# Splitting the input projection's weights in the transfers: two loads from the GpSimd queue, one rounding and one accumulating, in place of one load, casts and subtractions

## Chip, cores and metric

The kernel runs on 1 core of a Trainium2 chip. The metric is the device time of one execution in microseconds (us), the median of several. A profile of one execution stands beside the times.

## What is computed

One layer of a diffusion backbone, for 128 context tokens and 512 latent tokens of width 1024. All arithmetic is float32. What matters here is the first product of the token-mixing part:

```python
p = h @ w_in                       # (640, 1024) x (1024, 5664)
qkv, z, beta, a, sc, gates = jnp.split(p, SPLITS, axis=-1)
qkv = silu(conv_centred(qkv, conv_qkv, n_rows))
q, k, v = heads(...)               # 8 heads of 64, q and k normalised
o_f, s_f = gated_delta_chunked(q, k, v, beta[0], g[0], s0[:, 0])
o_b, s_b = gated_delta_chunked(fl(q), fl(k), fl(v), fl(beta[1]), fl(g[1]), s0[:, 1])
y_b = (bg * conv_centred(cg * xs, conv_sc, n_rows)) @ w_br_b
m = sigmoid(ga) * y_a + sigmoid(gb) * y_b
```

The chunked DeltaNet needs, for each chunk of 64 tokens, the inverse of a triangular matrix (`triangular_solve`), and then a scan over the chunks. After the mixing come an output projection and a SwiGLU network.

## The kernel before

**Products in two parts.** TensorE multiplies in a rounded float32 (`F32R`). To keep precision, each operand is split into a high part (the rounded value) and a low part (the rest, rounded too), and each product is made of three matmuls: high times high, high times low, low times high (`mm3`, lines 83 to 85).

**The input projection** has 45 weight tiles of 1024 x 128 (512 KB each). `load_w` (line 61) brings one tile into a raw buffer `wr` by a transfer from the queue of SyncE (SP). `split` (line 49) makes `wh` on ScalarE (ACT) by a cast and `wl` on VectorE (DVE) by subtracting `wh` from the raw tile, in two halves of 512 columns each: per tile two casts (line 57) and two subtractions (line 58). Both stand at a raised priority (offset 200000). There are two buffers each for `wr`, `wh` and `wl`. `gemm_cm` then multiplies the tile with the 640 tokens, in two halves of 320 tokens with 8 steps of depth and 3 matmuls each, 48 matmuls per tile. Tile 0 holds the columns for the decay (`gates`); `qkv`, `zgate`, `short` and `gate_th` use the other 44.

**The DeltaNet** works on 4 pairs of heads, one after the other. `prepare` (from line 407) normalises q and k, makes the factors and masks, and inverts the triangular matrices: on DVE, 30 dependent steps of a product (`otmp`, line 556) and a subtraction (`X`, line 558) on 32 x 32 blocks, then two transposes (`RT` and `R`, lines 562 and 563), whose results TensorE multiplies (line 575). GpSimd (POOL) makes masks (`em`, `ea`), scaled tiles (`qh`, `kl`), and fills the tiles `KU`, `RS` and `AQ` by elementwise work and by transfers of its own queue (lines 459 to 536). `scan` (from line 598) then goes over the chunks, with small matmuls from `KU`, `RS`, `EW` (line 640) and `AQ` (line 670).

**The order.** A scheduler places every instruction on its engine's queue by priority. `scan` has the highest (offset 300000), then the splits (200000), then `prepare` (1000), and the projection's tiles fill TensorE in between. Each engine works through its queue in order; an instruction that waits holds up all that stand behind it.

Of the kernel before, what the change touches and what calls it, by code (L numbers as in the profile page):

```python
# [9 lines left out]
F32 = mybir.dt.float32  # L10
F32R = mybir.dt.float32r
I32 = mybir.dt.int32
AF = mybir.ActivationFunctionType
ALU = mybir.AluOpType
# [4 lines left out]
P = 128  # L19
D = 1024  # L20
KT = D // P
# [16 lines left out]
class Kernel:  # L38
    def __init__(self, ctx, tc, ins, outs, dbg=None):
        self.tc, self.nc, self.ctx = tc, tc.nc, ctx  # L40
        self.I, self.O = ins, outs
        self.dbg = dbg or (lambda name, ap: None)


    def urgent(self):
# [15 lines left out]
    def load_w(self, src, shape, pool=None, urgent=True):  # L61
        raw = self.rpool.tile(shape, F32, name="wr", tag="wr", bufs=self.nraw)
        self.nc.sync.dma_start(out=raw, in_=src)
        return self.split(raw, shape, "w", pool, urgent=urgent)

    def rsqrt(self, out, x, pool, n, tag):

# [321 lines left out]
    def qkv(self, p, hT):  # L389

        nc = self.nc
        out = []
        for j in (1, 0, 2):
            w = self.load_w(self.I["w_in"][1 + 3 * p + j], [P, KT, P])
            i = 4 * j + p
            y = self.da.tile([P, TOK], F32, name="cm", tag="cm", bufs=4)
            for h in range(2):
                ps = self.gemm_cm(w, hT, h)
                o = h * HALF
                with self.urgent():  # L400
                    nc.scalar.activation(out=y[:, o:o + HALF], in_=ps, func=AF.Copy, scale=self.taps[:, 1, i:i + 1])
                    self.conv(ps, self.taps, i, y, o, 5, h == 0)
            nc.scalar.activation(out=y, in_=y, func=AF.Silu)
            out.append((j, y))
        return [y for _, y in sorted(out, key=lambda a: a[0])]


    def prepare(self, p, qkv):
        nc, dn, dc, g = self.nc, self.da, self.dc, self.g
        mm = nc.tensor.matmul  # L410
# [277 lines left out]

    def zgate(self, p, hT):
        nc = self.nc  # L690
        w = self.load_w(self.I["w_in"][13 + p], [P, KT, P])
        for h in range(2):
            s = slice(h * HALF, (h + 1) * HALF)
            ps = self.gemm_cm(w, hT, h)
            with self.urgent():
                nc.scalar.activation(out=self.zf[:, p, s], in_=ps, func=AF.Silu)

    def short(self, i, hT):
        nc = self.nc
        ab = self.ab  # L700
        wc = self.load_w(self.I["w_in"][17 + 3 * i], [P, KT, P])
        cx = ab.tile([P, TOK], F32, name="cx", tag="dt", bufs=2)
        y = ab.tile([P, TOK], F32, name="cy", tag="dt", bufs=2)
        for h in range(2):
            ps = self.gemm_cm(wc, hT, h)
            with self.urgent():
                nc.scalar.copy(out=cx[:, h * HALF:(h + 1) * HALF], in_=ps)
        wx = self.load_w(self.I["w_in"][18 + 3 * i], [P, KT, P])
        for h in range(2):
            s = slice(h * HALF, (h + 1) * HALF)  # L710
            ps = self.gemm_cm(wx, hT, h)
            with self.urgent():
                nc.vector.tensor_tensor(out=cx[:, s], in0=cx[:, s], in1=ps, op=ALU.mult)
        nc.vector.tensor_scalar(out=y, in0=cx, scalar1=self.tapsc[:, 1, i:i + 1], scalar2=None, op0=ALU.mult)
        self.conv(cx, self.tapsc, i, y, 0, 10, True)
        wb = self.load_w(self.I["w_in"][19 + 3 * i], [P, KT, P])
        for h in range(2):
            s = slice(h * HALF, (h + 1) * HALF)
            ps = self.gemm_cm(wb, hT, h)
            with self.urgent():  # L720
                nc.vector.tensor_tensor(out=y[:, s], in0=y[:, s], in1=ps, op=ALU.mult)  # L721
        nc.sync.dma_start(out=self.ybd[i], in_=y)

    def gate_th(self, i, hT):

        nc = self.nc
        w = self.load_w(self.I["w_in"][29 + i], [P, KT, P])
        t = self.ab.tile([P, TOK], F32, name="gt", tag="dt", bufs=2)
        for h in range(2):
            ps = self.gemm_cm(w, hT, h)  # L730
            with self.urgent():
                nc.scalar.activation(out=t[:, h * HALF:(h + 1) * HALF], in_=ps, func=AF.Tanh, scale=0.5)
        nc.sync.dma_start(out=self.thd[i], in_=t)
# [695 lines left out]
```

## Time and profile before

| | us |
|---|---|
| median of 3 runs | 1089.32 |
| lowest and highest run | 1086.92, 1091.1 |
| the profiled execution, its own time | 1085.4 |
| its span | 1083.6 |
| TensorE (PE) busy | 1024.1 |
| VectorE (DVE) busy | 835.8 |
| ScalarE (ACT) busy | 484.4 |
| GpSimd (POOL) busy | 138.9 |

The span runs from the first to the last instruction; 1.8 us of the execution lie around it. Busy times are unions of an engine's instructions. Matmuls are pipelined, so that a busy TensorE is not one at its peak. A wait is put down to the instruction that ended last before the waiting one could start. The input projection runs from 42 to 514 us of the span.

### The profile page before, as it was taken

To read this page: it belongs to the slowest core of one execution; us is meant where nothing else is said; L and a number is where in the kernel's file an instruction comes from. 1 tells how busy PE (TensorE), PEld (TensorE's weight loads), DVE (VectorE), ACT (ScalarE), POOL (GpSimd) and SP (SyncE) were. 2 spreads that over 40 slices of the span, in tenths; PEclk is the share of its full clock that TensorE was granted. 3 is DMA by queue.
4 is the path that set the end of the run, shared out by engine and by line. 5 is a ranking of instruction groups with operands and counts; after the bars stand their busy time and mean duration, and the time that the engine had idled before them with its cause. 6 is when DMAs were issued, how large, how long until landed. Compare 5 with 4: busy or idle time off the path is not lost.

```text
span 1083.6 us, 19702 instructions
## 1 busy us (share of the span) xinstructions
PE 1024.1 (95%) x7729; PEld 929.0 (86%) x7729; DVE 835.8 (77%) x1698; ACT 484.4 (45%) x929; POOL 138.9 (13%) x168
## 2 busy tenths in 40 slices
PE   6999978988988989999998998999999999999997
PEld 3699978887887888899996887999999999788885
DVE  5767896997898897995995789888777775975336
ACT  5568436417524324434223466444445444623321
POOL 2215321062062150101000000000000000000000
PEclk9999989998998999999998998999999999999999
DMA  9435712264164276547953532323222222552214
GB/s 343 147 91 135 206 52 67 72 152 113 42 164 125 68 171 202 182 151 246 318 167 116 185 108 89 103 85 98 94 79 78 98 81 76 177 173 96 81 39 156
DMA packets 47399, 141.52 MB, mean 131 GB/s; under 512 B 9517, under 2 KB 10034, under 8 KB 47306
## 3 DMA queue, kind: packets, MB, share of 16 engines
q1 hardware_dynamic: 42746, 127.10, 36.1%
q0 software_dynamic: 4560, 13.15, 5.4%
q8 instruction: 61, 1.00, 0.4%
q14 instruction: 32, 0.26, 0.1%
HBM read 117.57 MB, written 12.18 MB: 120 GB/s over the span
## 4 chain that ended last, share of the span: by engine, by line
PE 69%; DVE 14%; DMA 2%; ACT 2%; issue 2%; SPq 0%; DVEq 0%; POOL 0%; ACTq 0%
PE acc L1163 21%; PE d L84 7%; PE d L85 7%; PE d L83 7%; PE acc L84 6%; PE acc L83 6%; PE acc L85 6%; PE d L1163 3%; DVE X L558 3%; PE s L640 2%; DVE otmp L556 2%; DVE wl L58 1%; PE v L611 1%; PE v L670 1%; DMA ea<-scr 1%
## 5 line engine op out<-in xcount | busy, mean ns | idle before, releaser
L83 PE MATMUL d<-hT,wh 128*128 128x320 f32 x720 | 227.8, 317 | 1.2 <-DVE cy L721 1.1
L84 PE MATMUL d<-hT,wh 128*128 128x320 f32 x720 | 228.6, 318 | 0.0
L85 PE MATMUL d<-hT,wl 128*128 128x320 f32 x720 | 227.8, 317 | 0.4 <-DVE wl L58 0.4
L57 ACT CAST wh<-wr 128x512 fp32r<-128x512 f32 x150 | 87.8, 618 | 143.2 <-PE d L84 74.4
L83 PEld LDWEIGHTS d<-hT,wh 128*128 128x128 f32 x720 | 137.3, 191 | 3.9 <-DVE cy L721 1.7
L85 PEld LDWEIGHTS d<-hT,wl 128*128 128x128 f32 x720 | 137.3, 191 | 3.2 <-issue 0.7
L84 PEld LDWEIGHTS d<-hT,wh 128*128 128x128 f32 x720 | 137.1, 191 | 2.9 <-issue 0.3
L58 DVE TENSOR_TENSOR wl<-wr,wh 128x512 fp32r<-128x512 f32 x150 | 104.2, 717 | 36.4 <-ACT wh L57 35.2
L1163 PE MATMUL acc<-mh,wl 128*128 128x320 f32 x280 | 86.9, 310 | 1.8 <-DVE wl L1098 1.8
L83 PE MATMUL acc<-wh,as 128*128 128x512 f32 x220 | 85.7, 390 | 2.1 <-ACT as L1297 2.1
L1163 PE MATMUL acc<-mh,wh 128*128 128x320 f32 x280 | 87.0, 311 | 0.3 <-ACT early L1177 0.3
L196 DVE SCALAR_TENSOR_TENSOR gacc<-wr,cv,gacc 128x1024 f32<-128x1024 f32 x64 | 80.1, 1278 | 9.1 <-DMA wr<-in_w_mod_dram 7.2
L1163 PE MATMUL acc<-ml,wh 128*128 128x320 f32 x280 | 86.7, 310 | 0.0
L84 PE MATMUL acc<-wl,as 128*128 128x512 f32 x220 | 85.6, 389 | 0.0
L85 PE MATMUL acc<-wh,as 128*128 128x512 f32 x220 | 85.5, 389 | 0.0
L1102 ACT CAST wh<-wr 128x512 fp32r<-128x512 f32 x66 | 40.6, 622 | 72.0 <-PE acc L1163 37.0
L1102 ACT CAST wh<-S 128x512 fp32r<-128x512 f32 x88 | 54.1, 619 | 36.4 <-PE d L1163 19.6
L1098 DVE TENSOR_TENSOR wl<-S,wh 128x512 fp32r<-128x512 f32 x88 | 60.0, 686 | 3.9 <-ACT wh L1102 3.0
L1098 DVE TENSOR_TENSOR wl<-wr,wh 128x512 fp32r<-128x512 f32 x66 | 45.3, 689 | 19.1 <-ACT wh L1102 18.2
L1163 PEld LDWEIGHTS acc<-mh,wl 128*128 128x128 f32 x280 | 52.8, 188 | 2.1 <-DVE wl L1098 2.0
L1163 PEld LDWEIGHTS acc<-mh,wh 128*128 128x128 f32 x280 | 52.7, 188 | 0.6 <-ACT early L1177 0.6
L1163 PEld LDWEIGHTS acc<-ml,wh 128*128 128x128 f32 x280 | 52.8, 189 | 0.0
(365 smaller groups left out, 2348.9 us busy)
## 6 DMA issues: line engine op xcount, KB each, us to landing
wr<-in_w_ffn_in_dram SPq DMA_DIRECT2D x48, 512.0 KB, 3.7
wr<-in_w_in_dram SPq DMA_DIRECT2D x45, 512.0 KB, 3.5
wr<-in_w_mod_dram SPq DMA_DIRECT2D x32, 512.0 KB, 4.0
wr<-in_w_ffn_out_dram SPq DMA_DIRECT2D x22, 512.0 KB, 3.4
mr<-in_w_mod_dram SPq DMA_DIRECT2D x16, 512.0 KB, 8.5
thd<-gt SPq DMA_DIRECT2D x16, 320.0 KB, 4.1
bth<-thd SPq DMA_DIRECT2D x16, 320.0 KB, 3.0
wr<-in_w_br_dram SPq DMA_DIRECT2D x8, 512.0 KB, 6.9
```

Source lines behind the costliest of these rows:

```text
L57: (high or nc.scalar.copy)(out=hi[:, s], in_=raw[:, s])
L58: (low or nc.vector).tensor_tensor(out=lo[:, s], in0=raw[:, s], in1=hi[:, s].bitcast(F32), op=ALU.subtract)
L83: mm(out, lhsT=ah, rhs=bh, start=start, stop=False)
L84: mm(out, lhsT=ah, rhs=bl, start=False, stop=False)
L85: mm(out, lhsT=al, rhs=bh, start=False, stop=stop)
L196: nc.vector.scalar_tensor_tensor(out=acc[v], in0=w, scalar=self.cv[:, k, v:v + 1], in1=acc[v], op0=ALU.mult, op1=ALU.add)
L556: nc.vector.tensor_tensor(out=t, in0=B[:, j + 1:32, j:j + 1].broadcast_to([P, n, j]), in1=X[:, j:j + 1, 0:j].broadcast_to([P, n, j]), op=A ...
L558: nc.vector.tensor_tensor(out=X[:, j + 1:32, 0:j], in0=X[:, j + 1:32, 0:j], in1=t, op=ALU.subtract)
L640: mm(ps[half(c2), o:o + 64], lhsT=w(d, c2, t, hd), rhs=R[:, d, c2, t, hd, :], start=True, stop=True)
L1098: tt = lambda o, a, b, op: nc.vector.tensor_tensor(out=o, in0=a, in1=b, op=op)
L1102: nc.scalar.copy(out=dst[0], in_=src)
L1163: nc.tensor.matmul(ps, lhsT=A[x][:, k], rhs=B[y][:, k], start=start and k == 0 and n == 0, stop=k == 3 and n == 2, skip_group_check=True)
```

## The change

44 of the 45 weight tiles of the input projection (all but tile 0) come through a new function `load_parts`. It issues three instructions per tile:

1. a transfer from POOL's queue that reads the float32 weights and writes them rounded, as `wh` (called HI below);
2. on ACT, `wl` = -`wh`, one instruction of 1024 columns;
3. a second transfer from POOL's queue, that reads the same weights again and adds them into `wl` (called LO below).

The raw buffers are no longer needed for this, so every third tile puts its two parts into the two `wr` buffers: three pairs of buffers are in turn, where there were two.

```diff
@@ -40,6 +40,7 @@
         self.dbg = dbg or (lambda name, ap: None)
+        self.turn = itertools.count(1)
@@ -62,6 +63,17 @@
         return self.split(raw, shape, "w", pool, urgent=urgent)
+
+    def load_parts(self, src):
+
+        nc = self.nc
+        tags = ("wh", "wl") if next(self.turn) % 3 else ("wr", "wr")
+        hi, lo = (self.wpool.tile([P, KT, P], F32R, name=name, tag=tag) for name, tag in zip(("wh", "wl"), tags))
+        with self.tc.high_priority(offset=200000):
+            nc.gpsimd.dma_start(out=hi, in_=src)
+            nc.scalar.activation(out=lo, in_=hi.bitcast(F32), func=AF.Copy, scale=-1.0)
+            nc.gpsimd.dma_start(out=lo, in_=src, accum_op=ALU.add)
+        return hi, lo
@@ -391,7 +403,7 @@
-            w = self.load_w(self.I["w_in"][1 + 3 * p + j], [P, KT, P])
+            w = self.load_parts(self.I["w_in"][1 + 3 * p + j])
@@ -688,7 +700,7 @@
-        w = self.load_w(self.I["w_in"][13 + p], [P, KT, P])
+        w = self.load_parts(self.I["w_in"][13 + p])
@@ -698,14 +710,14 @@
-        wc = self.load_w(self.I["w_in"][17 + 3 * i], [P, KT, P])
+        wc = self.load_parts(self.I["w_in"][17 + 3 * i])
...
```

`...` stands for the same replacement in the rest of `short` and in `gate_th`. Lines behind `load_parts` stand 12 further down in the new file.

**DVE in the inversion of the third pair of heads.** Each row is one instruction of DVE's queue; `wl<-wr,wh` is a subtraction of the split. Before:

```order
L556 TENSOR_TENSOR otmp<-blk,X 128x210
L558 TENSOR_TENSOR X<-X,otmp 128x10x21
L556 TENSOR_TENSOR otmp<-blk,X 128x198
L58 TENSOR_TENSOR wl<-wr,wh 128x512
L558 TENSOR_TENSOR X<-X,otmp 128x9x22
L58 TENSOR_TENSOR wl<-wr,wh 128x512
L556 TENSOR_TENSOR otmp<-blk,X 128x184
L558 TENSOR_TENSOR X<-X,otmp 128x8x23
```

and now:

```order
L570 TENSOR_TENSOR X<-X,otmp 128x10x21
L697 SCALAR_TENSOR_TENSOR zf<-v,onorm,zf 128x640
L568 TENSOR_TENSOR otmp<-blk,X 128x198
L570 TENSOR_TENSOR X<-X,otmp 128x9x22
L568 TENSOR_TENSOR otmp<-blk,X 128x184
L570 TENSOR_TENSOR X<-X,otmp 128x8x23
```

The subtractions of the split are gone from between the dependent steps; other work of DVE (here `zf`) stays there.

**POOL where the scan of the first pair ends and the tiles of the second are filled.** `KU`, `RS` and `AQ` are the tiles that the scan reads; `wh<-in_w_in_dram` is HI, `wl<-in_w_in_dram` is LO. Before:

```order
L459 TENSOR_TENSOR KU<-ident,egl 64x640 x4
L471 DMA KU<-kl 64x2x640
L625 MEMSET RS 64x128 x2
L472 DMA RS<-bv 64x2x640
L471 DMA KU<-kl 64x2x640
L472 DMA RS<-bv 64x2x640
L490 DMA AQ<-qtT 64x5x64 x8
L536 DMA AQ<-ea 64x2x640 x2
```

and now:

```order
L73 DMA wh<-in_w_in_dram 128x1024
L75 DMA wl<-in_w_in_dram 128x1024
L73 DMA wh<-in_w_in_dram 128x1024
L75 DMA wl<-in_w_in_dram 128x1024
L471 TENSOR_TENSOR KU<-ident,egl 64x640 x4
L483 DMA KU<-kl 64x2x640
L637 MEMSET RS 64x128 x2
L484 DMA RS<-bv 64x2x640
L73 DMA wh<-in_w_in_dram 128x1024
L483 DMA KU<-kl 64x2x640
L484 DMA RS<-bv 64x2x640
L502 DMA AQ<-qtT 64x5x64
```

Loads of weight tiles now stand ahead of this work and in the midst of it. The first `KU` here waits for TensorE's last use of it in the scan, as before, and a HI and a LO stand behind that wait.

**POOL in the last tiles of the projection.** A HI and the LO behind it belong to one tile (buffers number n and n + 1). Before, POOL's queue had no load of weights here. Now:

```order
L73 DMA wh_5245<-in_w_in_dram 128x1024
L75 DMA wl_5246<-in_w_in_dram 128x1024
L73 DMA wh_5344<-in_w_in_dram 128x1024
L75 DMA wl_5345<-in_w_in_dram 128x1024
L73 DMA wh_5403<-in_w_in_dram 128x1024
L75 DMA wl_5404<-in_w_in_dram 128x1024
```

Each LO stands straight behind its own HI, and the next tile's HI behind that LO. A HI waits until TensorE has done with the tile three before it; a LO waits for ACT, and ACT for the HI's data.

## Rows read from the trace of the kernel before

**Rows 1.** The page: the line of the span, and part 1.
```profile
span 1083.6 us, 19702 instructions
...
PE 1024.1 (95%) x7729; PEld 929.0 (86%) x7729; DVE 835.8 (77%) x1698; ACT 484.4 (45%) x929; POOL 138.9 (13%) x168
```

**Rows 2.** Busy time by stretch; columns: stretch, length, engines, granted clock, DMA share, GB/s.
```profile
42.00:102.00 60.00, 59.44 (x435) 57.42 (x435) 40.82 (x94) 45.33 (x72) 17.40 (x18) 1.00 0.44 118
102.00:168.00 66.00, 57.70 (x422) 55.66 (x422) 62.06 (x147) 28.26 (x47) 22.77 (x23) 0.95 0.41 116
168.00:250.00 82.00, 72.40 (x864) 64.99 (x859) 70.67 (x165) 33.57 (x68) 21.59 (x25) 1.00 0.42 105
250.00:334.00 84.00, 76.29 (x870) 69.22 (x864) 72.24 (x172) 40.96 (x75) 26.06 (x30) 0.93 0.42 107
334.00:405.00 71.00, 66.62 (x843) 59.68 (x840) 61.64 (x138) 27.76 (x58) 25.06 (x29) 0.96 0.43 115
405.00:462.00 57.00, 56.23 (x681) 49.33 (x676) 47.66 (x77) 24.05 (x55) 3.81 (x5) 1.00 0.56 183
462.00:514.00 52.00, 51.97 (x350) 50.65 (x349) 39.38 (x48) 20.36 (x37) 5.68 (x7) 1.00 0.60 201
sum 472.00, PE 440.64 PEld 406.95 DVE 394.49 ACT 220.28 POOL 122.38; mean PE 62.95 PEld 58.14 DVE 56.36 ACT 31.47 POOL 17.48
```

**Rows 3.** Waits of PE, 42 to 514 us: total, times, longest.
```profile
PE v L575 <- DVE RT L562: 9.6, 4, 4.5
PE w L479 <- DVE kh L448: 7.4, 3, 5.9
PE v L670 <- DVE RS L644: 5.3, 3, 2.6
```

**Rows 4.** Groups of DVE and of ACT by form, 42 to 514 us.
```profile
L58 DVE TENSOR_TENSOR wl<-wr,wh 128x512 fp32r<-128x512 f32 x92 | 66.3, 737 | 13.9 <-ACT wh L57 13.2
...
L57 ACT CAST wh<-wr 128x512 fp32r<-128x512 f32 x91 | 54.2, 617 | 70.9 <-PE d L84 53.4 <-issue 9.2 <-DVE cy L721 4.3
```

**Rows 5.** Chain of waits, 42 to 514 us: shares by line, then single pieces.
```profile
by line: PE d L84 12.0%; PE d L85 11.5%; PE d L83 11.4%; DVE X L558 5.9%; PE s L640 5.2%; DVE otmp L556 4.8%; DVE wl L58 3.3%; issue 2.3%; PE v L611 2.2%; PE v L670 1.9%; DMA ea<-scr 1.8%; DVE RT L562 1.7%; DMA AQ<-ea 1.4%; PE w L528 1.3%; 
...
119.67 6.62 DMA AQ<-ea
...
152.42 0.63 ACT wh L57
...
407.53 1.14 ACT wh L57 x2
```

**Rows 6.** Busy time by stretch of the instructions that touch wl alone.
```profile
42.00:102.00 60.00, 35.88 (x116) 21.68 (x116) 11.87 (x16) 1.00 0.44 118
102.00:168.00 66.00, 34.97 (x108) 21.12 (x108) 10.70 (x14) 0.95 0.41 116
168.00:250.00 82.00, 33.32 (x106) 19.90 (x106) 9.52 (x14) 1.00 0.42 105
250.00:334.00 84.00, 33.80 (x105) 20.71 (x105) 9.87 (x14) 0.93 0.42 107
334.00:405.00 71.00, 29.28 (x91) 17.50 (x91) 8.47 (x12) 0.96 0.43 115
...
462.00:514.00 52.00, 34.56 (x112) 21.11 (x113) 9.20 (x14) 1.00 0.60 201
```

**Rows 7.** DMA issues: count, size, median us from issue to landing.
```profile
wr<-in_w_in_dram SPq DMA_DIRECT2D x45, 512.0 KB, 3.5
...
RS<-bv POOLq DMA_DIRECT2D x8, 320.0 KB, 5.7
...
x1d<-yt POOLq DMA_DIRECT2D x5, 512.0 KB, 3.2
```

**Rows 8.** POOL: issue time of one transfer (min/median/max), and its waits.
```profile
L1063 POOL DMA_DIRECT2D x1d<-yt x5: 532/534/577, 609.0 to 645.4; - x5
...
POOL KU L459 <- PE s L640: 93.9, 3, 36.1
```

More of the change, by code (lines that the diff above doesn't have):

```diff
@@ L707, in short @@
                 nc.scalar.copy(out=cx[:, h * HALF:(h + 1) * HALF], in_=ps)
-        wx = self.load_w(self.I["w_in"][18 + 3 * i], [P, KT, P])
+        wx = self.load_parts(self.I["w_in"][18 + 3 * i])
         for h in range(2):
@@ L715, in short @@
         self.conv(cx, self.tapsc, i, y, 0, 10, True)
-        wb = self.load_w(self.I["w_in"][19 + 3 * i], [P, KT, P])
+        wb = self.load_parts(self.I["w_in"][19 + 3 * i])
         for h in range(2):
@@ L726, in gate_th @@
         nc = self.nc
-        w = self.load_w(self.I["w_in"][29 + i], [P, KT, P])
+        w = self.load_parts(self.I["w_in"][29 + i])
         t = self.ab.tile([P, TOK], F32, name="gt", tag="dt", bufs=2)
```

## The prediction

> **What bounds the kernel now.** I read the page's first part first [rows 1]: TensorE is busy for 95% of the span. The change touches only the input projection, which runs from 42 to 514 us, so I cut that into stretches [rows 2]. The reader is to see two things there. TensorE is busy for 440.6 of these 472 us, which leaves 31.4 us of idle time as the most that better feeding could return, the clock apart. And the idle time lies in four stretches, from 102 to 405 us: 8.3, 9.6, 7.7 and 4.4 us (length less PE busy). These are the stretches in which DVE is busiest (62.1 of 66, 70.7 of 82, 72.2 of 84, 61.6 of 71 us); before and behind them TensorE is full.
>
> Next I asked what TensorE waits for [rows 3]. The three largest waits end on DVE, 22.3 us in all: on `RT`, the end of the inversion, on `kh`, and on `RS` in the scan. They are not waits for weights. So the weights' subtractions cost time only by standing in DVE's queue among the steps that lead to `RT` and `kh`. The chain of waits [rows 5] tells how much of them is on the path: 3.3% of 472 us.
>
> **What the change takes away.** The subtractions are 92 of 737 ns in the window [rows 4]; 88 belong to the changed tiles, 64.9 us of DVE. The 88 casts at 617 ns are 54.3 us of ACT. In the four stretches the subtractions take 10.7, 9.5, 9.9 and 8.5 us [rows 6], each more than TensorE's idle time there. But they are not all on the path: on the chain there are 3.3% of 472 us = 15.6 us of subtractions, and five pieces of casts, 0.5 to 1.1 us, 3.5 us together (the first and the last are in rows 5). I take these 19.1 us as the gain, and not the 38.6 us of all subtractions in the four stretches, since DVE itself has 3.9, 11.3, 11.8 and 9.4 us without work there: other releasers than DVE's load come next. What is late then is the inversion's own steps (`X` 5.9% and `otmp` 4.8% of the chain), which stay.
>
> **What it adds.** ACT: 44 negations of 1024 columns. The nearest row is the cast of 512 columns, 617 ns [rows 4], so 0.62 to 1.23 us each; I take 1.2, or 53 us. It stands in for 54.3 us and cancels. The cover is ACT's own slack: 220 of 472 us busy [rows 2].
>
> POOL: 88 issues. The nearest are its own transfers of a 128 x 1024 tile, 0.53 us [rows 8], together 47 us on an engine that is busy for 122 of 472 us. The raw loads leave SP's queue; its other transfers can only come earlier for it, which I price at nothing.
>
> The supply of weights is what could fail, since one POOL queue now does it in series. Per tile: HI from issue to landing, the negation, the issue of LO; only then comes the next HI. For HI the nearest row is the same tile loaded from SP's queue, 3.5 us, or 3.2 us for a tile of that size issued by POOL [rows 7]. So 3.5 + 1.2 + 0.5 = 5.2 us per tile if LO's landing lies wholly beside the next HI. If the next HI has to wait until LO is in, LO's landing comes on top. No row shows an accumulating transfer. The nearest by size is 3.2 to 3.5 us; the nearest that reads SBUF as LO must (`RS`, 320 KB, from POOL's queue) takes 5.7 us [rows 7]. So the series takes 5.2 to 8.7 us with the first, up to 10.9 us with the second.
>
> What TensorE wants is read from the matmuls with `wl`, 16 per tile [rows 6]: 7.0 tiles in the last stretch, or one per 7.4 us; 7.25 tiles in the first, one per 8.3 us; one per 9.8 us in the second; one per 12.4, 12.8 and 12.5 us in the next three. I take 7 us, the middle between 5.2 and 8.7, which is faster than any of these; even 8.7 us would cost 7.0 x 1.3 + 7.25 x 0.4, less one tile's lead of 7.4 us, or 5 us. I put down 3 us.
>
> Here a rule speaks against the change. The Trainium skill (Collectives: The Full Stack, "The bandwidth ceiling: the fold count and why AG ≠ RS ≠ AR") says that an add in the transfer path needs two source reads, and that reducing so runs at about half the rate of copying (62.28 against 32.35 GB/s there). By it LO would take up to twice a plain load's transfer, and the sum would be that of the supply rival below; no run here shows it yet.
>
> POOL's other work: `KU` stood in its queue waiting 93.9 us for the scan in three waits [rows 8], with everything behind it held. Loads now stand ahead of it, and a HI and a LO behind it; with three pairs of buffers two tiles are ahead, 25 us at the pace of that stretch, so I price this wait at nothing. The transfers to `RS` and `AQ`, which the next scan reads, come later by the loads between them. I put down 1 us; nothing bounds it but the rival below.
>
> **The sum.** Against the profiled execution's 1085.4 us: - 15.6 - 3.5 + 3 + 1 = 1070.3 us. The median of the runs lies 3.9 us above that execution, so **1074 us** as a median. From 514 us on TensorE's work is the same in the same order; I change nothing there.
>
> **The rivals.**
>
> *The path moves to POOL and the transfers; no change.* Between pairs of heads the chain runs through POOL: `AQ` is filled from `ea`, a transfer that takes 6.6 us [rows 5], then `ea` is loaded anew, and DVE waits for it. These transfers now stand in POOL's queue behind a HI that waits for TensorE, or a LO that waits for a landing. One landing of 3.5 us at each of four pairs gives back 14 us: 1085.4 - 19.1 + 14 + 3 + 3.9 = 1087 us. For it speaks that DVE already has idle time in these stretches; against it, that the scheduler puts most loads where POOL would have waited anyway.
>
> *The supply is too slow; slower.* If LO holds up the next HI for 5.7 us, the series takes 10.9 us. Then TensorE waits in the full stretches: 7.0 x (10.9 - 7.4) = 24.5 us in the last, less the one tile of lead, 7.4; 7.25 x 2.6 = 18.9 us in the first; 6.75 x 1.1 = 7.4 us in the second; nothing in the next three. Together 43.4 us, and 1085.4 - 19.1 + 43.4 + 3.9 = 1114 us. It decides from about 9.7 us per tile, where the loss (7.0 x 2.3 + 7.25 x 1.4 - 7.4 = 19 us) eats the gain. For it speaks the series in one queue, with each LO straight behind its own HI; against it the 3.2 us that a plain tile takes from the same queue.
>
> **How the numbers follow.** Forecast 0.60, no change 0.17, slow supply 0.23. A measurement of this kernel can tell some 0.5% from no change, here 5.4 us: 1083.9 to 1094.8. The forecast lies below that band for nearly all of its own spread (1050 to 1084), the first rival inside it or just below, the second above it. So faster 0.61, same 0.17, slower 0.22. The range's low end is the return of all 31.4 us of idle time, and some 8 of the 12 us that the granted clock (0.95, 0.93, 0.96 in three stretches of 66, 84 and 71 us [rows 2]) takes: 1085.4 - 39.4 + 3.9 = 1050. Its high end is the second rival's 1114; beyond these lie a LO over 5.7 us and little else.
>
> **What would show it.** Right: TensorE's waits for `RT` and `kh` shrink by more than half, DVE is busy for some 65 us less, no wait of TensorE names a transfer of `wl`, and the last stretch keeps 7.4 us per tile. Wrong: TensorE's low-part matmul (line 97 of the new file) waits for a landing, a LO takes over 6 us to land, the tiles of the last stretch come 9 us apart or more, or the waits for `RT` and `kh` stay while the chain goes through `AQ` and `ea`.

## The result and the profile after

The changed kernel takes **1173.03 us** (median of 4 runs, 1167.41 to 1174.85), against 1088.67 (4 runs, 1086.92 to 1091.1) for the kernel before, run beside it: a ratio of 1.0764, interval 1.074 to 1.0788. It is 84 us slower, where 1074 us had been forecast. Every run lies above 1114, the high end of the range.

The page of the changed kernel: the line of the span, part 1, and from part 3 the two queues' packets, MB and share.

```profile
span 1173.0 us, 19624 instructions
...
PE 1049.8 (89%) x7729; PEld 949.6 (81%) x7729; DVE 778.7 (66%) x1610; ACT 482.1 (41%) x884; POOL 205.1 (17%) x256
...
q1 hardware_dynamic: 36410, 104.03, 27.0%
q0 software_dynamic: 17232, 59.30, 23.5%
```

DVE is busy for 57 us less than in [rows 1], as the change meant. TensorE does the same 7729 matmuls, and is busy for 26 us longer. The q0 queue is the one that POOL issues to; it now moves the weights, twice.

The stretches of the changed kernel, cut at the start of TensorE's first product with `RT` of each pair; the projection now ends at 604 us.

```profile
43.00:206.00 163.00, 132.17 (x876) 125.98 (x875) 85.37 (x212) 76.58 (x108) 63.36 (x71) 0.91 0.62 139
206.00:286.00 80.00, 71.62 (x824) 63.62 (x824) 56.15 (x149) 30.40 (x55) 21.86 (x27) 0.94 0.53 117
286.00:373.00 87.00, 71.40 (x828) 64.52 (x828) 64.71 (x158) 37.31 (x65) 35.42 (x41) 0.94 0.63 136
373.00:457.00 84.00, 71.89 (x788) 64.01 (x789) 53.93 (x125) 28.12 (x52) 36.27 (x44) 0.86 0.67 146
457.00:604.00 147.00, 120.53 (x1102) 110.60 (x1101) 78.94 (x106) 44.96 (x82) 30.46 (x41) 0.94 0.76 212
sum 561.00, PE 467.62 PEld 428.73 DVE 339.10 ACT 217.36 POOL 187.37; mean PE 93.52 PEld 85.75 DVE 67.82 ACT 43.47 POOL 37.47
```

The stretches of [rows 2] end at the same events: 126 us (its first two together), 82, 84, 71 and 109 (its last two). So the stretch ahead of the first inversion is 37 us longer, the three cycles are -2, 3 and 13 us longer, and the stretch behind the last is 38 us longer: 89 us, all within the projection. The stretches don't hold the same tiles: counted by their matmuls, 14.0, 6.6, 6.5, 5.7 and 12.1 before, and 15.1, 5.9, 6.0, 5.6 and 12.5 now, so that part of the 37 us is a tile that moved there from the cycles. (The two profiled executions are 89 us apart, 1174.85 and 1085.4 us; the medians 84.) TensorE's idle time there is 561.0 - 467.6 = 93.4 us, against 31.4 in [rows 2], so 62 us of the loss is idle time. The other 27 is busy time, for the same matmuls at a lower granted clock (0.86 to 0.94, before 0.93 to 1.00; such a mean is a mix of the full 2.4 GHz and 1.2 GHz): a matmul of the projection takes 327 to 328 ns on average, where it took 317 to 318. The first and the last stretch are those in which TensorE had been full.

What the engines waited for, 43 to 604 us of the changed kernel (total, times, longest):

```profile
PE w L491 <- DVE kh L460: 13.4, 3, 6.8
PE d L97 <- DMA wl<-in_w_in_dram: 13.3, 6, 5.9
PE m L220 <- ACT cph L58: 9.8, 2, 6.4
PE v L623 <- DVE EW L604: 9.8, 2, 5.2
PE v L598 <- ACT Y L592: 8.0, 3, 3.2
...
PE v L587 <- DVE RT L574: 5.2, 4, 2.6
...
POOL wl L75 <- ACT wl L74: 186.8, 32, 11.1
POOL wh L73 <- PE d L97: 64.5, 18, 8.4
...
ACT wl L74 <- DMA wh<-in_w_in_dram: 117.4, 32, 11.1
...
DVE cm L391 <- ACT cm L413: 35.5, 14, 7.0
```

TensorE itself waits for a landing of `wl` for 13.3 us only. The long waits stand one engine further back: POOL in LO, for ACT's negation; ACT in the negation, for HI's landing; and DVE for ACT's `cm` (35.5 us, before 7.2). TensorE's wait for `kh` grew against [rows 3], though DVE had less to do; its wait for `RT` shrank. Such a list tells where engines stand, not what each standing costs; the runs below ask that.

The three instructions per tile as groups, over the whole run (busy time, mean ns of one, idle time before them), then the transfers from issue to landing, 43 to 604 us:

```profile
L74 ACT ACTIVATE wl<-wh 128x1024 fp32r<-128x1024 f32 x44 | 46.6, 1059 | 118.4 <-DMA wh<-in_w_in_dram 117.4 <-DVE wl L59 0.9
L75 POOL DMA_DIRECT2D wl<-in_w_in_dram x44 | 40.0, 909 | 234.1 <-ACT wl L74 186.8 <-ACT RS L656 17.9 <-ACT gt L744 13.4
L73 POOL DMA_DIRECT2D wh<-in_w_in_dram x44 | 30.0, 682 | 76.2 <-PE d L97 64.5 <-PE d L96 11.7
```

```profile
wl<-in_w_in_dram POOLq DMA_DIRECT2D x44, 512.0 KB, 5.7
wh<-in_w_in_dram POOLq DMA_DIRECT2D x42, 512.0 KB, 6.2
...
RS<-bv POOLq DMA_DIRECT2D x8, 320.0 KB, 7.2
```

HI needs 6.2 us to land, where [rows 7] had 3.5 for the same tile from SP's queue. `RS` needs 7.2, where it had 5.7.

POOL's queue in the first stretch of the changed kernel (start, duration, instruction, idle time before it and what ended that), and below it ACT's negations of the same tiles:

```profile
85.24 0.88 POOL L75 DMA_DIRECT2D wl<-in_w_in_dram  x1 [6.38 <-ACT wl L74]
85.80 0.88 POOL L73 DMA_DIRECT2D wh<-in_w_in_dram  x1
90.75 1.27 POOL L512 TENSOR_TENSOR ea<-ea,G 128x640 f32<-128x640 f32 x1 [4.08 <-DMA ea<-scr]
...
95.30 0.89 POOL L75 DMA_DIRECT2D wl<-in_w_in_dram  x1 [1.59 <-ACT wl L74]
...
98.29 0.58 POOL L73 DMA_DIRECT2D wh<-in_w_in_dram  x1
...
106.22 0.97 POOL L75 DMA_DIRECT2D wl<-in_w_in_dram  x1 [5.67 <-ACT wl L74]
106.83 0.94 POOL L73 DMA_DIRECT2D wh<-in_w_in_dram  x1
...
93.94 1.06 ACT L74 ACTIVATE wl<-wh 128x1024 fp32r<-128x1024 f32 x1 [1.87 <-DMA wh<-in_w_in_dram]
104.86 1.06 ACT L74 ACTIVATE wl<-wh 128x1024 fp32r<-128x1024 f32 x1 [2.49 <-DMA wh<-in_w_in_dram]
```

This is one turn of the series: HI issued at 85.80, its negation at 93.94 (8.1 us later), LO at 95.30; the next HI at 98.29, its negation at 104.86, LO at 106.22. From LO to LO it is 10.1 and 10.9 us. The 3.0 us between the LO at 95.30 and the next HI hold POOL's own work for the DeltaNet. TensorE took a tile per 9.0 us in this stretch before (14.0 tiles ahead of the first product with `RT`, counted by their matmuls, in 125.6 us), and per 10.8 us now (15.1 tiles in 163.5 us). The last seven tiles of the projection came 10.6 us apart (74.4 us for the seven), where they had come 7.3 us apart (51.4).

### The profile page after: what moved, and what is told of

Read it like the earlier page. It is cut to its first block, busy times and chain, and to the rows that moved or that the text cites. A ratio compares the mean times of both kernels' runs of the same rounds, so it can differ in the third digit from the quotient of the medians.

```text
span 1173.0 us, 19624 instructions
## 1 busy us (share of the span) xinstructions
PE 1049.8 (89%) x7729; PEld 949.6 (81%) x7729; DVE 778.7 (66%) x1610; ACT 482.1 (41%) x884; POOL 205.1 (17%) x256
## 3 DMA queue, kind: packets, MB, share of 16 engines
q0 software_dynamic: 17232, 59.30, 23.5%
## 4 chain that ended last, share of the span: by engine, by line
PE 42%; issue 4%; DVE 4%; DMA 2%; ACT 1%; POOL 1%; DVEq 0%; POOLq 0%; ACTq 0%
PE acc L1175 19%; PE acc L97 5%; PE acc L96 5%; PE acc L95 5%; PE d L1175 3%; PE d L97 2%; PE d L95 2%; PE d L96 2%; DMA wl<-in_w_in_dram 1%; DMA wr<-in_w_ffn_in_dram 0%; DMA cscr<-crow 0%; DVE wl L1110 0%; DVE hq L1110 0%; DMA x1d<-yt 0%; DVE yt L1074 0%
## 5 line engine op out<-in xcount | busy, mean ns | idle before, releaser
L97 PE MATMUL d<-hT,wl 128*128 128x320 f32 x720 | 235.5, 328 | 13.6 <-DMA wl<-in_w_in_dram 13.3
L95 PE MATMUL d<-hT,wh 128*128 128x320 f32 x720 | 235.4, 327 | 2.2 <-ACT cx L719 1.5
L96 PE MATMUL d<-hT,wh 128*128 128x320 f32 x720 | 235.2, 327 | 0.8 <-DVE hT L824 0.8
L97 PEld LDWEIGHTS d<-hT,wl 128*128 128x128 f32 x720 | 143.3, 199 | 18.7 <-DMA wl<-in_w_in_dram 14.8
L95 PEld LDWEIGHTS d<-hT,wh 128*128 128x128 f32 x720 | 143.3, 199 | 6.0 <-issue 1.8
L96 PEld LDWEIGHTS d<-hT,wh 128*128 128x128 f32 x720 | 143.8, 200 | 4.2 <-DVE hT L824 1.6
L74 ACT ACTIVATE wl<-wh 128x1024 fp32r<-128x1024 f32 x44 | 46.6, 1059 | 118.4 <-DMA wh<-in_w_in_dram 117.4
L75 POOL DMA_DIRECT2D wl<-in_w_in_dram x44 | 40.0, 909 | 234.1 <-ACT wl L74 186.8
L1114 ACT CAST wh<-wr 128x512 fp32r<-128x512 f32 x66 | 40.8, 625 | 72.1 <-PE acc L1175 36.9
L58 ACT CAST wh<-wr 128x512 fp32r<-128x512 f32 x62 | 35.6, 620 | 74.9 <-PE d L96 23.8
L59 DVE TENSOR_TENSOR wl<-wr,wh 128x512 fp32r<-128x512 f32 x62 | 40.6, 689 | 29.3 <-ACT wh L58 28.8
L1110 DVE TENSOR_TENSOR wl<-wr,wh 128x512 fp32r<-128x512 f32 x66 | 45.4, 690 | 19.4 <-ACT wh L1114 18.5
L202 POOL MEMSET gacc<- 128x1024 f32 x8 | 7.9, 1053 | 276.7 <-PE acc L1175 274.4
```

The source lines that it names most:

```text
L58: (high or nc.scalar.copy)(out=hi[:, s], in_=raw[:, s])
L59: (low or nc.vector).tensor_tensor(out=lo[:, s], in0=raw[:, s], in1=hi[:, s].bitcast(F32), op=ALU.subtract)
L74: nc.scalar.activation(out=lo, in_=hi.bitcast(F32), func=AF.Copy, scale=-1.0)
L75: nc.gpsimd.dma_start(out=lo, in_=src, accum_op=ALU.add)
L95: mm(out, lhsT=ah, rhs=bh, start=start, stop=False)
L96: mm(out, lhsT=ah, rhs=bl, start=False, stop=False)
```

## The experiments

The letters in the expectations are these theories. **S**: the series of landing, negation and accumulating landing is too long. **B**, later **Q**: ACT and POOL stand in their waits, and their DeltaNet work comes late. **C**: a tile is loaded twice, and the transfers' bytes cost. **G**: VectorE's subtractions were what TensorE waited for, as predicted, and taking them away gains. **N**: it gains nothing.

**First: depth, the negation's engine, and each half alone.** In the first run two pairs of buffers take turns in place of three:

```diff
-        tags = ("wh", "wl") if next(self.turn) % 3 else ("wr", "wr")
+        tags = ("wh", "wl")
```

> The change with two pairs of buffers in place of three (no tile uses the raw buffers). Theory S (the series is too long): from the moment that TensorE frees a pair, HI takes 6.2 us to land, the negation 1.1, LO 5.7, and the two issues 1.5, together 14.5 us; three pairs give two tiles of TensorE's work for it (14.8 us in the full stretches), two pairs give one (7.4 us). So each tile of a full stretch comes 7 us later, some 20 such tiles: 1173 + 140 = about 1310 us, and TensorE's waits that name wl rise from 13 us to over 100. Theory B (ACT and POOL stand still for the loads, and the DeltaNet's work behind them comes late; the weights are in time otherwise): the blocked time per tile stays, 1173 to 1200 us. Theory C (more bytes in the same 16 engines): the bytes are the same, 1165 to 1180 us.

Measured: 1218.0 us, ratio 1.1178 (1.1055 to 1.1301). S asked for far more, B and C for less. TensorE's waits in this run:

```profile
PE d L97 <- DMA wl<-in_w_in_dram: 76.2, 24, 7.5
```

So weights can come too late here, and with three pairs they mostly don't (13.3 us).

The second run negates on POOL, in its own queue:

```diff
-            nc.scalar.activation(out=lo, in_=hi.bitcast(F32), func=AF.Copy, scale=-1.0)
+            nc.gpsimd.tensor_scalar(out=lo, in0=hi.bitcast(F32), scalar1=-1.0, scalar2=None, op0=ALU.mult)
```

> The change with the negation on POOL in place of ACT, so that ACT never waits for HI (117 us of waits with the change). Theory B, with ACT as the engine that matters: most of these waits were in front of work that the DeltaNet needs, so 1173 goes down by 30 to 60 us, to 1115 to 1145. Theory B with POOL as the engine that matters: POOL stood in the same wait anyway (187 us for ACT), so 1165 to 1185. Theory S: the series gets longer by what POOL takes more for a negation than ACT's 1.06 us (about 1 to 2 us per tile): 1180 to 1210. Theory C: 1173, nothing changes.

Measured: 1219.07 us, 1.1188 (1.1129 to 1.1246), slower than any theory said. ACT no longer stands in the negation, but the run doesn't tell what that is worth: POOL's negation takes nearly three times ACT's and stands in the series, and TensorE's waits for `wl` rise to 48.9 us. The negation in this run:

```profile
L74 POOL TENSOR_SCALAR wl<-wh 128x1024 fp32r<-128x1024 f32 x44 | 130.1, 2957 | 198.9 <-DMA wh<-in_w_in_dram 168.7 <-issue 21.9 <-PE s L652 6.6
```

The third and the fourth run make one half of the change each. Both keep the raw load by SP, so that two pairs are left. One takes HI from POOL's transfer and subtracts on DVE; the other casts on ACT and takes LO from the accumulating transfer:

```diff
+        nc.sync.dma_start(out=raw, in_=src)
...
+            nc.gpsimd.dma_start(out=hi, in_=src)
+            for s in (slice(0, 4), slice(4, 8)):
+                nc.vector.tensor_tensor(out=lo[:, s], in0=raw[:, s], in1=hi[:, s].bitcast(F32), op=ALU.subtract)
```

> One part alone: HI comes by the rounding transfer of POOL's queue, the raw tile by SP's queue as before, and DVE subtracts in two halves as before; no negation, no LO, two buffers each. The casts leave ACT. The bytes moved per tile are twice those of before, as with the change. Theory C (bytes): most of the change's 84 us, 1130 to 1170. Theory S: the series is HI (3.7 to 6.2 us) and two subtractions (1.4 us), 5 to 8 us against one tile's 7.4 us: within or little over, 1085 to 1115. Theory B: ACT waits for no load any more and POOL for PE alone, but DVE now waits for HI: 1085 to 1115.

```diff
+        nc.sync.dma_start(out=raw, in_=src)
...
+            for s in (slice(0, 4), slice(4, 8)):
+                nc.scalar.copy(out=hi[:, s], in_=raw[:, s])
+            nc.scalar.activation(out=lo, in_=hi.bitcast(F32), func=AF.Copy, scale=-1.0)
+            nc.gpsimd.dma_start(out=lo, in_=src, accum_op=ALU.add)
```

> The other part alone: the raw tile by SP's queue and HI by ACT's two casts as before, then ACT negates HI, and POOL accumulates the weights into LO; no subtraction on DVE, two buffers each. ACT waits for no transfer of POOL's queue. Theory S: from TensorE's release, casts 1.2, negation 1.1, LO's issue and landing 6.6, together 9 us against 7.4 us in some 20 tiles of full stretches, 30 us, less the 15 us that DVE's relief gives: 1095 to 1115. Theory B: ACT is held only by TensorE, as before; POOL is held for ACT: 1075 to 1100. Theory C: the bytes are those of the change (raw, LO's two reads): 1130 to 1170.

Measured: 1150.16 us (1.0555, 1.0501 to 1.0609) and 1148.21 us (1.0537, 1.0435 to 1.064). Both lie where C put them, but each also has a pair less than the change, and the first run priced that pair at 45 us with the whole change. They don't tell bytes from depth, so the runs below take single costs out instead.

**Is there a gain at all?** The kernel before without its subtractions, and then with a quarter of each subtraction's columns (the diffs show lines that `load_parts` has in these runs):

```diff
+        nc.sync.dma_start(out=raw, in_=src)
...
+            for s in (slice(0, 4), slice(4, 8)):
+                nc.scalar.copy(out=hi[:, s], in_=raw[:, s])
+        return hi, hi
```

> The kernel before without its 88 subtractions in the projection: the low part is the high part itself, so the output is not the reference's; loads, casts and TensorE's work are as before, and VectorE loses 65 us. It is the gain that the change was predicted to make, without its transfers. G (VectorE is what TensorE waits for, and the subtractions stand in its way): 1065 to 1075. N (VectorE's lateness is the latency of the DeltaNet's own chain, which the subtractions only fill in): 1083 to 1092.

```diff
...
+                nc.vector.tensor_tensor(out=x[:, s], in0=raw[:, s, 0:32], in1=hi[:, s, 0:32].bitcast(F32), op=ALU.subtract)
+        return hi, hi
```

> The kernel before with each subtraction cut to 32 of 128 columns of each block and written to a scratch tile, the high part standing for the low (the output is not the reference's); VectorE keeps every instruction and its waits, at less work, and the order of TensorE's instructions differs from that of the run without subtractions. If the nothing that run gained was an accident of its order: 1070 to 1080. If VectorE's work is not what TensorE waits for: 1084 to 1092.

Measured: 1088.76 us, ratio **1.0** (0.9983 to 1.0018), and 1083.52 us, ratio 0.9952 (0.993 to 0.9974). So 65 us of subtractions less, or three quarters of their columns, give between nothing and 5 us: the first is N's figure, the second lies just below the second of its two ranges. In the run without subtractions, the sum of the stretches from 42 to 517 us, and what TensorE waited for:

```profile
sum 475.00, PE 442.02 PEld 408.52 DVE 347.08 ACT 216.04 POOL 126.04; mean PE 88.40 PEld 81.70 DVE 69.42 ACT 43.21 POOL 25.21
```

```profile
PE w L491 <- DVE kh L460: 6.5, 3, 4.7
PE v L587 <- DVE RT L574: 6.2, 2, 4.4
PE v L682 <- DVE RS L656: 4.0, 2, 2.3
PE s L652 <- DVE RS L656: 3.8, 2, 3.6
```

DVE is down from 394.5 to 347.1 us, and TensorE's idle time is 475.0 - 442.0 = 33.0 us, where it was 31.4. The waits for `kh`, `RT` and `RS` (line 682) fall from 22.3 us in [rows 3] to 16.7, and another wait for `RS` (line 652, 3.8 us) comes up. The inversion does come earlier: the first `RT` is used at 148 us, where it was 168. But the scheduler then puts only 11.4 tiles ahead of it, not 14.0, and TensorE makes the others at the end. TensorE's order is a new one in both runs, so what they price is the kernel that the scheduler makes without this work; no run takes the subtractions out of the old order.

A third way to relieve DVE adds no transfer: the first half of each subtraction goes to POOL.

```diff
+            for s, e in ((slice(0, 4), nc.gpsimd), (slice(4, 8), nc.vector)):
+                nc.scalar.copy(out=hi[:, s], in_=raw[:, s])
+                e.tensor_tensor(out=lo[:, s], in0=raw[:, s], in1=hi[:, s].bitcast(F32), op=ALU.subtract)
```

> The kernel before with the first half of each tile's subtraction on POOL and the second on VectorE: VectorE is relieved of 33 us without one more transfer. G: 1075 to 1083. N: 1085 to 1100, with POOL's slower subtraction as the new wait in the full stretches.

Measured: 1123.56 us, 1.0323 (1.0295 to 1.0351), slower than both. The groups of this run:

```profile
L76 POOL TENSOR_TENSOR wl<-wr,wh 128x512 fp32r<-128x512 f32 x44 | 61.7, 1403 | 225.0 <-ACT wh L75 209.4 <-PE d L98 10.1 <-DMA wr<-in_w_in_dram 4.9
...
L76 DVE TENSOR_TENSOR wl<-wr,wh 128x512 fp32r<-128x512 f32 x44 | 47.1, 1071 | 20.9 <-ACT wh L75 20.3 <-PE d L98 0.3
```

DVE's halves take 1071 ns each, against 737 in [rows 4], with POOL's subtraction of the other half beside them. So this run doesn't price DVE's relief by itself.

**Bytes.** The kernel before with an extra load per tile from SP's queue into a tile that nobody reads, of 7/8 and then of 3/8 of the weights:

```diff
         w = self.load_w(src, [P, KT, P])
+        x = self.xpool.tile([P, 7, P], F32, name="wx", tag="wx")
+        with self.tc.high_priority(offset=200000):
+            self.nc.sync.dma_start(out=x, in_=src[:, 0:7])
         return w
```

> The kernel before with an extra load of 7/8 of each weight tile from SP's queue into a tile that nobody reads: the bytes of the second load alone, with no work on POOL, no negation and no wait. C: 1120 to 1150, since each half of the change alone, with its one more load per tile, cost 59 us. S and Q: within 10 us of the kernel before, 1085 to 1100.

> The kernel before with an extra load of 3/8 of each weight tile from SP's queue into two alternating scratch tiles, so that no transfer waits for the one before it. The run with 7/8 and one scratch tile took 1114 us, 26 us more, and SP stood 113 us for that tile. If the bytes cost: 3/7 of 26, or 1096 to 1103. If SP's standing did: 1086 to 1093.

Measured: 1114.04 us (1.024, 1.0194 to 1.0285) and 1100.12 us (1.0092, 1.0064 to 1.0119). The first lies between the figures of C and of the others, the second where the bytes put it. That is 26 us for 7/8 and 10 us for 3/8, in proportion to the bytes as far as the intervals tell. With it the raw tile itself lands later, which is the first line of each run, and SP stands for the scratch tile, which is the second:

```profile
wr<-in_w_in_dram SPq DMA_DIRECT2D x45, 512.0 KB, 6.6
...
SPq L73 <- DMA wx<-in_w_in_dram: 113.0, 36, 7.8
```

```profile
wr<-in_w_in_dram SPq DMA_DIRECT2D x45, 512.0 KB, 7.1
...
SPq L73 <- DMA wx<-in_w_in_dram: 46.6, 29, 6.3
```

SP's standing fell in the same proportion as the bytes (46.6 of 113.0 us), so these two runs don't separate them. Nor does the cost follow the raw tile's landing, which is later with the smaller load (7.1 us) than with the larger (6.6). TensorE's order changed in both, and its share is not known either. Next, loads in POOL's queue: the change with the second load plain and no negation (two free loads), and one rounding load alone that serves as both parts.

```diff
             nc.gpsimd.dma_start(out=hi, in_=src)
-            nc.scalar.activation(out=lo, in_=hi.bitcast(F32), func=AF.Copy, scale=-1.0)
-            nc.gpsimd.dma_start(out=lo, in_=src, accum_op=ALU.add)
+            nc.gpsimd.dma_start(out=lo, in_=src)
```

> Both loads by POOL, rounding, the second one plain and with no negation in between, so the low part holds the whole weights and the output is not the reference's: the two transfers of a tile wait for TensorE's release of the pair alone and run beside each other. S: the series is one landing of about 6 us and three pairs cover it, 1060 to 1095. Q: POOL's queue is still held, now by the wait for TensorE's release alone (in the run with the rounding transfer alone it stood 211.7 us there and the time was 1150), 1135 to 1155. C: the same two loads per tile, 1125 to 1150.

> One rounding transfer by POOL per tile, used as high and as low part (the output is not the reference's): no casts, no subtractions, no negation, the bytes of the kernel before, six tiles deep. G: 1055 to 1072. N: 1083 to 1095. Q (any load in POOL's queue holds POOL's DeltaNet work): 1100 to 1130. With the run that has two such loads at 1114, C asks for about 26 us less than that, 1085 to 1092.

Measured: 1113.98 us (1.0241, 1.0188 to 1.0294) and 1103.83 us (1.0136, 1.0108 to 1.0163). For the two loads all three figures missed. On the single load only Q's figure holds, though its mechanism, POOL standing, turns out below to cost nothing. With the bytes of the kernel before, no split at all and six tiles of depth it is 15 us slower than before, and its own wait for `RT` is 17.0 us. So of the 26 us of two free loads, 15 come with the first one, in POOL's queue and in another order of instructions, and 10 with the second, which also halves the depth and changes the order again.

**Who stands.** POOL's queue held without a load: the kernel before with two one-column subtractions per tile on POOL that wait for the casts.

> The kernel before with two subtractions of one column per tile on POOL, in the loads' place in its order, each waiting for one cast of the tile: POOL's queue is held until the high parts are there, at most one pair ahead of TensorE, with no bytes and hardly any work. Q: POOL's other work (the copies and products of the DeltaNet, the x1 transfers) comes late as in the two halves of the change, 1115 to 1150. S and C: 1085 to 1100.

Two free loads again, with one column's subtraction on POOL between them, which waits for HI; then with one column's copy on ACT instead, that waits for HI:

> The run without a negation (two free transfers, plain second one, low part equal to the weights, so the output is not the reference's; 1114 us) with one column's subtraction on POOL between the two loads, which waits for the rounding transfer: POOL's queue is held for each landing, as in the change, with ScalarE free and TensorE's order that of that run. If the 26 us between that run and the plain one with the negation (1140 us) come from POOL standing and the second load coming late: 1132 to 1145. If from ScalarE standing in the negation: 1110 to 1120.

> The same run with one column's copy on ScalarE that waits for the rounding transfer, in the negation's place in its order: ScalarE stands as in the change, POOL and the second load do not wait for it (the output is not the reference's). If ScalarE's standing is what costs: 1132 to 1145. If it is POOL's standing and the late second load: 1110 to 1120.

Measured: 1088.42 us (1.0006, 0.9986 to 1.0026), 1111.81 us (1.0217, 1.0182 to 1.0252) and 1106.66 us (1.0155, 1.0119 to 1.019), the last two to be held against the 1.0241 of two free loads. The waits of POOL in the first and in the second of these runs:

```profile
POOL wx L74 <- ACT wh L58: 203.0, 55, 14.4
```

```profile
POOL wx L75 <- DMA wh<-in_w_in_dram: 140.6, 39, 6.4
```

TensorE's order is the same in each of these two runs, but for a few matmuls, as in the one it is compared with. POOL stands for 203.0 and 140.6 us, and no cost shows: the ratios agree within their intervals. In the second of them the plain second load also comes late, behind HI's landing, and that costs nothing either. In the third ACT stands for 66.9 us (117.4 in the change), and the time doesn't rise; but TensorE's order is another there, so this shows only that such a standing need not cost.

**The accumulate and the wait for it.** The change with a plain second load behind the true negation; the change with the negation reading a constant, so that LO need not wait for HI; and both edits together.

```diff
-            nc.gpsimd.dma_start(out=lo, in_=src, accum_op=ALU.add)
+            nc.gpsimd.dma_start(out=lo, in_=src)
```

> The change with the second transfer of each tile written plainly in place of accumulated, so the low part holds the whole weights and the output is not the reference's: same two loads, same negation, same waits, without the accumulate's second read of the weight tile. In the changed kernel the 4096-byte packets of the accumulating transfer took 327 ns against 159 to 174 ns of the others, and its landing 5.7 us. S (the series load, negate, accumulate of one tile sets the rate, about 10.5 us per tile in the stretch 85 to 160 us): each tile loses some 1.7 to 2 us of its series; over the 12 to 20 tiles that are waited for that is 20 to 40 us, so 1130 to 1153. Q (POOL's queue is held by the accumulate's wait for the negation, and the DeltaNet's own POOL and ScalarE work comes late): POOL waits for the negation as before, 1155 to 1173. C (the bytes of the second load slow the other transfers): the engine time of the accumulate halves, from 59 MB's worth at double price on half of it, 1140 to 1160.

```diff
-            nc.scalar.activation(out=lo, in_=hi.bitcast(F32), func=AF.Copy, scale=-1.0)
+            nc.scalar.activation(out=lo, in_=self.ones.unsqueeze(1).to_broadcast([P, KT, P]), func=AF.Copy, scale=-1.0)
```

> The change with ScalarE writing the low tile from a constant instead of from the rounded weights, so the accumulating transfer no longer waits for the rounding one (the output is not the reference's): same bytes, same two reads of the accumulate, same ScalarE time, the series broken. S (the series carries the accumulate's price): 1114 to 1130, near the run without a negation. C (the accumulate's second read slows all transfers, whoever waits): 1140 to 1150, that run plus the 33 us that the plain second load gave back.

> The run whose negation reads a constant and whose second load accumulates (1141 us), with that second load plain (output not the reference's): the same order of TensorE, ScalarE's 1.06 us per tile kept, nobody waits for the rounding transfer. It is the fourth corner beside no negation at all (1114), the plain second load behind the true negation (1140) and the change (1173). If the accumulate's second read costs by itself: 1110 to 1120, so that it is worth some 27 us with no wait for it in the series. If ScalarE's own 47 us of writing cost the 27: 1135 to 1145.

Measured, as medians (ratios and intervals in brackets):

| | second load plain | second load accumulating |
|---|---|---|
| negation reads a constant | 1118.25 (1.0275, 1.0239 to 1.031) | 1141.05 (1.0482, 1.045 to 1.0513) |
| negation waits for HI | 1139.87 (1.0463, 1.0407 to 1.0519) | 1173.03 (1.0764, 1.074 to 1.0788) |

TensorE's order is the same within each row of the table, but for a few matmuls, so its steps to the right are the accumulate's own price: 23 and 33 us. It is paid where nothing waits for HI, too; there C's figure holds (1140 to 1150), and S's doesn't. Its steps down, 22 and 32 us, hold the wait and a new order in one: with the wait TensorE meets the first `RT` after 15.1 tiles, without it after 11.9. What the accumulate does, in the page's queue line and the landing of `wl` of the plain run in the lower row:

```profile
q0 software_dynamic: 17232, 59.30, 19.1%
```

```profile
wl<-in_w_in_dram POOLq DMA_DIRECT2D x44, 512.0 KB, 4.0
```

The packets and bytes are those of the change, which has 23.5%. Per engine that is 0.235 x 1173.0 - 0.191 x 1142.1 = 57.5 us more, or 920 us over 16 engines, which for the 44 x 128 packets of 4 KB is 163 ns each. In the traces most of the accumulating packets take about 327 ns and most plain ones of that size about 174. Without the accumulate LO's landing is 1.7 us shorter (4.0 for 5.7), and HI's is too, by 1.4 (4.8 for 6.2): with the true negation in between, the accumulate lengthens both landings of the series.

Last, ACT's standing and work together, but with LO not behind them: ACT negates 7/8 of the tile into a scratch tile, and the second load is plain.

> Two loads by POOL, the second plain, and the negation of 7/8 of the tile written to a scratch tile: ScalarE waits for the rounding transfer and does the work as in the change, but the second load does not wait for it (output not the reference's). With one column's wait the time was 1107, with the whole negation ahead of the second load 1140. If ScalarE's standing plus work cost the 26 to 33 us: 1130 to 1145. If it is the second load that comes late behind landing and negation: 1105 to 1118.

Measured: 1122.34 us, 1.0301 (1.0271 to 1.0332), in between, and nearer to the 1118 of the free pair than to the 1140 with LO behind the negation. It meets the first `RT` after 15.3 tiles, so the later place of the inversion alone doesn't explain the 1140. The 18 us between these two runs come with LO behind the negation, but the two orders differ in much else, and a LO late behind HI's landing alone cost nothing above. What the lateness of LO costs by itself is not shown.

No run points to a version faster than both. The most that a DVE without subtractions gave is 5 us, and every way of making the parts elsewhere cost more.

## Why the prediction was wrong

**The gain, -15.6 - 3.5 us: wrong.** It was read off the chain of waits: 3.3% of 472 us of subtractions and 3.5 us of casts, taken as time that goes when they go. The run without subtractions gave 0.0 us (at most 2, by its interval), the one with a quarter of their columns 5 (at most 8). The 3.5 us of casts were taken out by no run alone. The first step, that DVE is what TensorE waits for, holds as a reading of [rows 3]. The second, that the subtractions therefore stand in the way, gave no time back: without them the waits change places, and the idle time stays at 33 us. That the inversion's own dependent steps hold these waits, and that the scheduler moves TensorE's tiles along, is how I read it; it is not shown.

**The supply, +3 us: wrong in kind and size.** HI was taken at 3.5 us and landed after 6.2; with the measured negation and LO issue the inner series is 6.2 + 1.06 + 0.91 = 8.2 us, where I took 5.2 as the lower bound and 7 as the value; POOL's own work stands in the queue on top of it. From LO to LO it was 10.1 and 10.9 us. This lies above the 9.7 us from which the slow-supply rival was to decide, and near its 10.9. The rival had the sign, and in the last seven tiles its size too: they took 23 us longer, where it had 24.5, or 17.1 after one tile's lead. But only 9.5 of these 23 are waits for `wl`; 6.4 are a wait for ACT's cast of `cph`, 1.5 one for ACT's `cx`, and the rest is longer busy time. Over the whole its figure of 1114 was still 59 us short. It kept the gain of 19.1 us, which isn't there; it priced waits for `wl` alone, of which TensorE has 13.3 us; and of the stretches in which it said "nothing", the last cycle lost 13 us. What the supply cost is told by the runs: taking the accumulate out gave back 33 us, taking out the wait for HI 32 us (with a new order).

**The clock, at nothing.** The sum and its rivals had no term for a lower clock; I counted only what a higher one might return. 27 of the 89 us between the two profiles are busy time of TensorE for the same matmuls. By length times what the granted clock lacks, an estimate, the lower clock takes up to 12 us in the stretches of [rows 2] and up to 45 us in those above.

**The rule on the add: right, and I set it aside.** I cited the rule from the Trainium skill (Collectives: The Full Stack, "The bandwidth ceiling: the fold count and why AG ≠ RS ≠ AR") that an add in the transfer path needs two source reads. The runs agree with it: a packet of the accumulating load takes 163 ns more at the same bytes, and the accumulate alone costs 23 to 33 us. I said that by the rule the sum would be the supply rival's; in fact twice a plain landing of 3.5 us is 7.0, and the series would have been up to 12.2 us by that estimate, over the rival's 10.9. The measured landing was 5.7.

**ACT's negation "cancels": right as work.** 1059 ns was measured for 1.2 taken, and writing the low tile from a constant moved the time of two free loads by 4 us, which is within the intervals. The cover that I named, ACT's slack, hid the work. It did not hide LO, which comes only when ACT has reached the negation.

**POOL's issues, 47 us beside other work, and the `KU` wait at nothing.** LO's issue took 0.91 us, HI's 0.68, for 0.53 taken: 70 us. That standing of POOL costs nothing is what the runs found, though I argued it from depth: 203 us of it left the kernel before at a ratio of 1.0006. The +1 us for the path through `RS` and `AQ` is priced by no run alone; it is part of what loads in POOL's queue cost.

**The no-change rival** put 14 us on the DeltaNet's transfers standing behind a HI or a LO in POOL's queue. POOL did stand, and in the runs above that cost nothing. What the trace shows is another thing, that such a transfer itself takes longer (`RS` from 5.7 to 7.2 us).

**My signs.** Of the signs of being wrong, two came: the low-part matmul waits for a landing (13.3 us), and the last tiles come 10.6 us apart. LO's landing stayed under 6 us. DVE did lose 57 of the 65 us, and the wait for `kh` grew all the same.

**The ledger by runs**, in medians over 1088: two free loads in POOL's queue, with casts and subtractions gone, +26 (15 with the first, 10 with the second); ACT writing the low tile, +4; the accumulate, +23; the wait for HI and the order that comes with it, +32. Each step starts from the run before it, so that they add up to the measured 84 by construction. The +4 is within the intervals, and the runs of one step were not all taken beside each other. In the other order the last two are +22 and +33. Not settled: how much of the 15 us of one load in POOL's queue is the load and how much the new order; the same for the wait; what the lateness of LO costs by itself; and which transfer carries the price of the second load.

## What to carry to other kernels

An instruction on the chain of waits is worth its time only if no other chain is as long: before paying for its removal, run the kernel without it and see whether the idle time of the engine that sets the end goes. A load split into two that depend on each other through a third engine adds up landings, and here most of the waiting appeared on the helper engines, not on the engine that is fed. Expect an accumulating transfer to take more time at the same bytes (here 163 ns more per packet of 4 KB), and look at what a second read of the weights does to the landings beside it.

## What was not expected of the hardware

- POOL's record of issuing the accumulating transfer lasts 909 ns on average (905 with a constant), where that of the plain one of the same shape lasts 541 (the run with a constant and a plain second load; 554 behind the true negation). The next issue can start before it is over, 0.56 us after it began at 85.24 in the rows above. Line 75 of the plain run:

```profile
L75 POOL DMA_DIRECT2D wl<-in_w_in_dram x44 | 23.8, 541 | 45.6 <-ACT wl L74 41.4 <-issue 2.3 <-ACT RS L656 1.0
```

- DVE's subtraction of 512 columns went from 737 to 1071 ns with POOL's subtraction beside it. In the trace 23 of the 44 begin while one of POOL's runs and end 0.55 to 0.56 us after it; most of those that meet none take 0.67 to 0.69 us. The Trainium skill (SBUF — State Buffer, "SBUF: two separate sides") says that the two share a pair of ports, which the one that starts first locks for its whole instruction while the other waits; the durations agree with it.
- POOL needed 2957 ns for the negation that ACT does in 1059.
